# Moving pairs of operand slabs of an MLP to different addresses modulo 256

## The chip, the cores and the metric

The kernel runs on one core of one Trainium2 chip. The metric is the device time of one execution in microseconds (us); lower is better. The kernel before takes 698.64 us (median of 3 runs, 698.64 to 700.39). One more execution was profiled; it took 700.27 us, of which the profile shows a span of 698.4 us. The engines are named as in the profile: PE is the matrix engine (its weight loads are shown apart as PEld), DVE the vector engine, ACT the scalar engine, POOL the general-purpose engine, SP the engine whose queue issues most of the transfers.

## The reference

One layer of a decoder for 512 tokens of width 1024 in float32. Cut to what matters here:

```python
u = rms_norm(h, attn_pre_norm)
proj = u @ w_in                                   # two groups of heads: gated DeltaNet, block attention
mix = concatenate([o_gdn, o_moba]) @ w_out
h = h + rms_norm(mix, attn_post_norm)
f = square(relu(rms_norm(h, mlp_pre_norm) @ w_up)) @ w_down      # the MLP, inner width 4096
h = h + rms_norm(f, mlp_post_norm)
h = h + sigmoid(h @ w_ple_gate) * (p @ w_ple)
```

The change touches only the storage of operands in the MLP (the line with `w_up` and `w_down`) and in the last gate product (`w_ple_gate`).

## The kernel before

**Split operands.** A float32 operand is held as two tiles in the matrix engine's reduced type (F32R in the code, fp32r in the profile): `hi` is a cast of it by ACT, `lo` is the rest, by a subtraction on DVE. `split` (L672 to L677) does this: the cast is L675, the subtraction L676. `mm3` (L181 to L185) makes one product of two such pairs as three matmuls into one accumulator: hi by hi (L182), then hi by lo and lo by hi (both L185). Its first operand `l` is stationary (loaded as weights, 128 columns), its second, `r`, is moving (512 columns as a rule, 256 or 260 in a few places). Every matmul has its own weight load.

**The front part** (to about 262 us) is the input projection and both groups of heads. Its weights are loaded in chunks by `load_w` (L152) into rings of four `hi` and four `lo` tiles of 1040 floats each, one chunk of 8 k-tiles after the other. A tile has 4160 bytes in each partition, 16 times 256 and 64 more, so the tiles of a ring do not all start at the same address modulo 256. In the program as it is allocated the four take the starts 224, 160, 96 and 32 (modulo 256) turn by turn, `hi` and `lo` of one chunk always the same. These weight chunks are the stationary operand of the projections `pc`, `pmk`, `pmq` and `pz`; the moving one is `uT`, which starts at 224 modulo 256. Every slice of these operands that one matmul reads begins a multiple of 512 bytes further on, so it has the same address modulo 256 as its tile.

| operand (front part) | address modulo 256 |
|---|---|
| moving: `uT` hi and lo | 224 |
| stationary, chunk of `pmk2`, `pmq2` | 224 |
| stationary, chunk of `pmk3`, `pmq3` | 160 |
| stationary, chunk of `pmk0`, `pmq0` | 96 |
| stationary, chunk of `pmk1`, `pmq1` | 32 |

`pmk0` to `pmk3` and `pmq0` to `pmq3` are the keys and queries of the second group of heads, 24 matmuls each, in this order. `wv` is the one group of the front with 260 columns: there `uT` is stationary and the weights move, at many different addresses modulo 256 (steps of 16).

**The MLP.** Its operands lie in slabs of 1024 floats (4096 bytes in each partition). The class `Slabs` (L630) keeps a list of free slabs for each of two types: `sf` for float32 (raw weights and intermediate results), `sr` for F32R (all split operands). `more` (L634) makes new ones, `take` takes the first of the list, `give` puts slabs back at its end; so slabs are used in turn, and a slab's next writer waits for the matmuls that read it last. `sr` gets its slabs at three places: R_LEFT = 11 in a pool on the left side of the memory, R_RIGHT = 4 in a pool on the right side once the front's pools are closed (L749), and R_LATE = 12 (L850) over the space of the raw `w_down` tiles and of `f0`, when the main loop is over. The allocator rounds the size of every tile up to a multiple of 32 bytes.

As 4096 is a multiple of 256, all 27 `sr` slabs have the same address modulo 256, namely 224, and so have the moving operands `u2T` and `h2T` (both are in the place of `uT`). The slices that a matmul reads begin at multiples of 512 bytes inside a slab.

Products of this part, all through `mm3`:

- `up` (L757), 32 blocks: stationary is a split pair of `w_up`, moving is `u2T`. The first four blocks run as two halves of 256 columns each, the other 28 with 512. Output tiles are called `pu`.
- `product` (L804), 7 times for each of three quarters of the inner width (a Strassen scheme, 21 products in all): stationary is a split pair of activations `fs`, moving are two split pairs of `w_down`, 24 matmuls of 512. Output tiles are called `pd`. After each product `next_up` runs one block of `up`, so the order on PE is 24 matmuls of `pd`, 24 of `pu`, and so on; one `product` and one `up` take 8 slabs in turn.
- the last quarter, from L885: activations `f_hl` (four split pairs, held from their making to the end) by `w_down` slabs `wd` (8 pairs), 192 matmuls.
- the gate, from L903: stationary is `h2T`, moving are split pairs of `w_ple_gate`, 168 matmuls of 512 and 48 of 256. Output tiles are called `pg`.

The order of instructions on each engine is made by the framework's scheduler from the program order and the dependences. Casts and subtractions for coming products are issued as soon as their slabs come free, one to two products ahead of PE.

Of the kernel before, what the change touches and what calls it, by code (L numbers as in the profile page):

```python
# [10 lines left out]
F32R = mybir.dt.float32r  # L11
# [4 lines left out]
P = 128  # L16
T = 512
NT = T // P
D = 1024
# [11 lines left out]
BLK = 32  # L31
LVL = (32, 64)

F_LEFT, R_LEFT, R_RIGHT, R_LATE = 12, 11, 4, 12


K_ID = 0
# [31 lines left out]
def hybrid_layer(ctx: ExitStack, tc: tile.TileContext, x, p, w_in, w_tok, w_out, w_up, w_down, w_ple, w_gate,  # L69
# [560 lines left out]
    class Slabs:  # L630
# [2 lines left out]

        def more(self, n, pool):  # L634
            for _ in range(n):
                self.free.append(pool.tile([P, D], self.dt, name=f"{self.name}{self.made}"))
                self.made += 1

        def take(self):
# [157 lines left out]
    for g in range(NS):  # L797
        f = F[g % 2]
# [166 lines left out]
```

## Time and profile before

| what | before |
|---|---|
| median of 3 runs | 698.64 us |
| profiled execution | 700.27 us |
| its span | 698.4 us |
| PE busy | 682.5 us (98% of the span) |
| DVE busy | 439.0 us (63%) |
| ACT busy | 324.5 us (46%) |
| front part, 0 to 262 us: PE busy | 256.83 us |
| output projection, 262 to 302 us: PE busy | 38.57 us of 40 |
| first blocks of `up`, 302 to 350 us: PE busy | 47.05 us of 48 |
| Strassen products with `up`, 350 to 595 us: PE busy | 245.00 us of 245 |
| last quarter, 595 to 644 us: PE busy | 47.20 us of 49 |
| gate, 644 to 698 us: PE busy | 47.83 us of 54 |

How to read it: matmuls are pipelined in the profile, a row gives 390 ns for one of 512 columns, but the next one starts about 227 ns after it. So the rate of PE is read from the distance between starts in the timeline, not from the duration in a row. Where PE is busy all the time, every nanosecond between two starts is a nanosecond of the total.

### The profile page before, as it was taken

Reading aid. Unit: us, or ns where it says so; the run is one execution under the profiler, and the core shown is the slowest. Engines: PE = TensorE matmul, PEld = TensorE weight load, DVE = VectorE, ACT = ScalarE, POOL = GpSimd, SP = SyncE. Lnnn points to the kernel's source line nnn. Section 1 sums busy time; section 2 is a strip of 40 time slices with the busy share of each in tenths; the row PEclk is TensorE's granted clock in tenths of the full one; section 3 lists DMA queues with packets and bytes.
Section 4 is the critical chain, followed back from the end, with each engine's and each line's share of the span. In section 5 each row is a group of like instructions: output and inputs, shape, how many; then the busy total and the mean of one; then the engine's idle time right before and its main releaser. Section 6 shows DMA issues by size and latency. Waiting matters only on the chain. (4 is left out here: it accounts for less than half of the span.)

```text
span 698.4 us, 9002 instructions
## 1 busy us (share of the span) xinstructions
PE 682.5 (98%) x3418; PEld 564.8 (81%) x3418; DVE 439.0 (63%) x687; ACT 324.5 (46%) x598; POOL 48.6 (7%) x91
## 2 busy tenths in 40 slices
PE   8999999999999999999999999999999999999897
PEld 5998888888877768789888888888888888678786
DVE  4748889367676655675386456955778756634532
ACT  6536343433466655445265644454335454523311
POOL 1401100000011100230000000000000000032100
PEclk9999999999999999999999999999999999999999
DMA  8732323532102028286004440154211124544421
GB/s 331 301 122 61 101 86 105 114 109 92 31 31 61 31 61 309 112 258 255 31 31 150 122 150 31 61 151 151 90 35 56 61 76 136 184 84 121 122 77 47
DMA packets 38556, 79.24 MB, mean 113 GB/s; under 512 B 9776, under 2 KB 10416, under 8 KB 38512
## 3 DMA queue, kind: packets, MB, share of 16 engines
q1 hardware_dynamic: 36640, 74.98, 32.7%
q0 software_dynamic: 1152, 2.10, 1.9%
q10 hardware_dynamic: 720, 1.57, 0.6%
q8 instruction: 27, 0.44, 0.3%
q14 instruction: 17, 0.14, 0.1%
HBM read 70.51 MB, written 7.08 MB: 111 GB/s over the span
## 5 line engine op out<-in xcount | busy, mean ns | idle before, releaser
L185 PE MATMUL pd<-sr,sr 128*128 128x512 f32 x464 | 143.6, 390 | 0.6 <-DVE sr L676 0.5
L185 PE MATMUL pu<-u2Tl,sr 128*128 128x512 f32 (+1 forms) x288 | 105.4, 366 | 0.7 <-DVE u2Tl L198 0.7
L182 PE MATMUL pu<-u2Th,sr 128*128 128x512 f32 (+1 forms) x288 | 105.4, 366 | 0.0
L185 PE MATMUL pu<-u2Th,sr 128*128 128x512 f32 (+1 forms) x288 | 105.2, 365 | 0.0
L185 PEld LDWEIGHTS pd<-sr,sr 128*128 128x128 f32 x464 | 86.9, 188 | 19.8 <-DVE sr L676 1.7
L182 PE MATMUL pd<-sr,sr 128*128 128x512 f32 x232 | 90.7, 391 | 0.5 <-ACT sr L675 0.5
L676 DVE TENSOR_TENSOR sr<-sf,sr 128x1024 fp32r<-128x1024 f32 x48 | 58.6, 1222 | 38.5 <-ACT sr L675 14.9
L676 DVE TENSOR_TENSOR sr<-wd,sr 128x1024 fp32r<-128x1024 f32 x42 | 51.3, 1222 | 29.6 <-PE pu L185 28.1
L770 ACT ACTIVATE f<-pu 128x512 f32<-128x512 f32 (+1 forms) x36 | 19.9, 552 | 95.7 <-PE pu L185 95.7
L675 ACT CAST sr<-sf 128x1024 fp32r<-128x1024 f32 x48 | 50.3, 1047 | 27.3 <-DMA sf<-in_w_ple_gate 11.9
L185 PEld LDWEIGHTS pu<-u2Tl,sr 128*128 128x128 f32 x288 | 54.3, 189 | 9.7 <-DVE u2Tl L198 0.9
L185 PEld LDWEIGHTS pu<-u2Th,sr 128*128 128x128 f32 x288 | 54.3, 189 | 8.8
L182 PEld LDWEIGHTS pu<-u2Th,sr 128*128 128x128 f32 x288 | 54.3, 189 | 8.6
L675 ACT CAST sr<-wd 128x1024 fp32r<-128x1024 f32 x42 | 44.2, 1051 | 19.4 <-PE pd L185 19.4
L182 PEld LDWEIGHTS pd<-sr,sr 128*128 128x128 f32 x232 | 43.6, 188 | 10.1 <-ACT sr L675 1.4
L182 PE MATMUL pc<-uTh,w_h 128*128 128x512 f32 x96 | 39.3, 409 | 0.0
L185 PE MATMUL pc<-uTh,w_l 128*128 128x512 f32 x96 | 38.6, 402 | 0.0
L185 PE MATMUL pc<-uTl,w_h 128*128 128x512 f32 x96 | 38.5, 401 | 0.0
L825 DVE TENSOR_TENSOR sf<-sf,pd 128x512 f32<-128x512 f32 x28 | 19.1, 685 | 22.2 <-PE pd L185 22.2
L830 DVE TENSOR_TENSOR wd<-wd,wd 128x1024 f32<-128x1024 f32 x24 | 29.3, 1223 | 0.6
L182 PE MATMUL pg<-sr,h2Th 128*128 128x512 f32 (+1 forms) x72 | 27.2, 377 | 0.0
L185 PE MATMUL pg<-sr,h2Th 128*128 128x512 f32 (+1 forms) x72 | 27.0, 376 | 0.0
(421 smaller groups left out, 1324.2 us busy)
## 6 DMA issues: line engine op xcount, KB each, us to landing
sf<-in_w_up SPq DMA_DIRECT2D x32, 512.0 KB, 3.3
wd<-in_w_down SPq DMA_DIRECT2D x24, 512.0 KB, 4.7
w_r<-in_w_in SPq DMA_DIRECT2D x12, 512.0 KB, 3.6
wo_r<-in_w_out SPq DMA_DIRECT2D x8, 512.0 KB, 3.7
sf<-in_w_ple_gate SPq DMA_DIRECT2D x8, 512.0 KB, 4.3
sf<-in_w_down SPq DMA_DIRECT2D x8, 512.0 KB, 4.3
wv_r<-in_w_tok SPq DMA_DIRECT2D x4, 520.0 KB, 6.6
x<-in_x SPq DMA_DIRECT2D x4, 512.0 KB, 6.9
```

What stands on the lines that cost most here:

```text
L182: nc.tensor.matmul(dst, l[0], r[0], start=start, stop=False)
L185: nc.tensor.matmul(dst, a, b, start=False, stop=stop and i == 1)
L675: nc.scalar.copy(hi, src)
L676: nc.vector.tensor_sub(lo, src, hi.bitcast(F32))
L770: nc.scalar.activation(fq[:, side, c0:c1], pt[:, :n], AF.Relu)
L825: add(dst, dst, pts[j])
L830: sub(B[dst + (kk,)], B[x_ + (kk,)], B[y_ + (kk,)])
```

## The change

`R_LEFT` goes from 11 to 10, so that all three groups of `sr` slabs have even sizes (10, 4, 12) and a split pair always takes two neighbours of one group. The second slab of each pair is made wider than the 1024 floats that are used, by the difference of two neighbours in a list of 13 offsets, modulo 256 bytes. The pair behind it thereby starts at another address modulo 256. Nothing else changes: the same instructions on the same shapes, with one slab less.

```diff
-F_LEFT, R_LEFT, R_RIGHT, R_LATE = 12, 11, 4, 12
+F_LEFT, R_LEFT, R_RIGHT, R_LATE = 12, 10, 4, 12
+SKEW = (0, 64, 128, 32, 16, 96, 192, 48, 160, 80, 112, 224, 240)
...
         def more(self, n, pool):
             for _ in range(n):
-                self.free.append(pool.tile([P, D], self.dt, name=f"{self.name}{self.made}"))
+                wide = 0
+                if self.dt == F32R and self.made % 2:
+                    i = self.made // 2
+                    wide = (SKEW[(i + 1) % len(SKEW)] - SKEW[i]) % 256 // 4
+                self.free.append(pool.tile([P, D + wide], self.dt, name=f"{self.name}{self.made}")[:, 0:D])
                 self.made += 1
```

## The prediction

> **What bounds the kernel now.** I read the page first, then busy time by stage, then PE's waits in the MLP, then its timeline. The page and the table by stage (columns: us, then busy us and count of PE, PEld, DVE, ACT, POOL, granted clock, DMA share, GB/s):
>
> ```profile
> PE 682.5 (98%) x3418; PEld 564.8 (81%) x3418; DVE 439.0 (63%) x687; ACT 324.5 (46%) x598; POOL 48.6 (7%) x91
> ...
> 350.00:595.00 245.00, 245.00 (x1083) 202.85 (x1082) 165.15 (x160) 120.38 (x144) 0.00 (x0) 1.00 0.30 94
> 595.00:644.00 49.00, 47.20 (x211) 37.57 (x210) 25.62 (x29) 19.79 (x31) 9.25 (x15) 1.00 0.48 121
> 644.00:698.00 54.00, 47.83 (x234) 39.98 (x232) 19.29 (x28) 10.94 (x18) 2.83 (x5) 0.96 0.30 91
> ```
>
> From 350 to 595 us PE is busy for 245.00 of 245 us at full clock. PE's waits between 302 and 600 us are these two, both before 320 us:
>
> ```profile
> PE pu L185 <- DVE u2Tl L198: 0.7, 1, 0.7
> PE u L206 <- PE pu L185: 0.3, 1, 0.3
> ```
>
> So the MLP costs the number of its matmuls times the distance between two starts, and only a change of that distance, or a new wait, can move the time. The distance is read from the timeline (start, duration, engine, line). Rows of L182 are every third matmul:
>
> ```profile
> 383.21 0.39 PE L182 MATMUL pd<-sr,sr 128*128 128x512 f32 x1
> ...
> 388.65 0.39 PE L182 MATMUL pu<-u2Th,sr 128*128 128x512 f32 x1
> ```
>
> One Strassen product: 24 starts in 5.44 us, 226.7 ns each. All its operands start at 224 modulo 256. The front part has the comparison that this change calls for, the same shape with `uT` moving from 224 and a stationary chunk from other addresses:
>
> ```profile
> 97.10 0.39 PE L182 MATMUL pmk<-uTh,wmk_h 128*128 128x512 f32 x1
> ...
> 100.60 0.39 PE L182 MATMUL pmk<-uTh,wmk_h 128*128 128x512 f32 x1
> ...
> 107.46 0.39 PE L182 MATMUL pmk<-uTh,wmk_h 128*128 128x512 f32 x1
> ...
> 111.58 0.39 PE L182 MATMUL pmk<-uTh,wmk_h 128*128 128x512 f32 x1
> 112.27 0.40 PE L182 MATMUL pmq<-uTh,wmq_h 128*128 128x512 f32 x1
> ...
> 117.15 0.40 PE L182 MATMUL pmq<-uTh,wmq_h 128*128 128x512 f32 x1
> ...
> 124.15 0.39 PE L182 MATMUL pmq<-uTh,wmq_h 128*128 128x512 f32 x1
> ...
> 128.91 0.39 PE L182 MATMUL pmq<-uTh,wmq_h 128*128 128x512 f32 x1
> ```
>
> Call *distance* the start of the next matmul's stationary operand minus the start of the present one's moving operand, modulo 256 (the next weights load while the present matmul runs). The chunks in turn: `pmk1`, stationary at 32, distance 64: 15 starts in 3.50 us, 233.3 ns. `pmk3`, at 160, distance 192: 18 in 4.12 us, 228.9 ns. `pmq0`, at 96, distance 128: 21 in 4.88 us, 232.4 ns. `pmq2`, at 224, distance 0: 21 in 4.76 us, 226.7 ns, as in the MLP. The rate changes with the chunk's tile and comes back with it. Equal addresses are the fastest of the four cases; the others cost 6.7 (64), 5.7 (128) and 2.2 ns (192) more per matmul.
>
> **What the change does to the addresses.** The pads in bytes are 64, 64, 160, 240, 80 in the left group, 96, 112 in the right one, 112, 176, 32, 112, 16, 16 in the late one. Sizes are rounded up to 32, so 240 counts 256, 80 counts 96, 112 counts 128, 176 counts 192 and 16 counts 32. The left group still begins at 224, so its five pairs start at 224, 32, 96, 0, 0. The right group ends where it ended and is 224 bytes longer, so it begins at 0: pairs at 0 and 96. The late group is below it, at 224, 96, 32, 64, 192, 224. They don't all differ: three pairs of the main loop start at 0. `u2T` and `h2T` stay at 224.
>
> Walking the free list through the program (a product takes three pairs, a block of `up` one, of seven in turn) gives the distance of each 512-wide matmul on a slab. Their numbers are from these groups (mean duration overlaps the next matmul):
>
> ```profile
> L185 PE MATMUL pd<-sr,sr 128*128 128x512 f32 x464 | 143.6, 390 | 0.6 <-DVE sr L676 0.5
> L182 PE MATMUL pd<-sr,sr 128*128 128x512 f32 x232 | 90.7, 391 | 0.5 <-ACT sr L675 0.5
> L182 PE MATMUL pu<-u2Th,sr 128*128 128x512 f32 x224 | 87.1, 389 | 0.0
> ...
> L182 PE MATMUL pg<-sr,h2Th 128*128 128x512 f32 x56 | 22.6, 404 | 0.0
> ```
>
> 464 + 232 `pd`, 3 x 224 `pu` and 3 x 56 `pg` are 1536. Of them 261 keep distance 0, 170 get 64, 377 get 128, 103 get 192; 375 get 32 (286 of them `pu`, whose slab is at 0 against `u2T` at 224), 85 get 96, 129 get 160, 36 get 224.
>
> *Priced distances.* 170 x 6.7 + 377 x 5.7 + 103 x 2.2 ns = 1.14 + 2.15 + 0.23 = 3.5 us more, all on PE where it never waits.
>
> *Unpriced distances* (32, 96, 160, 224; 625 matmuls). Upper bound: the dearest row, 6.7 ns each, 4.2 us. Lower bound, a gain: that of a matmul without any overhead. Compare matmuls of 256 and 260 columns:
>
> ```profile
> 302.44 0.28 PE L182 MATMUL pu<-u2Th,sr 128*128 128x256 f32 x1
> ...
> 304.96 0.28 PE L182 MATMUL pu<-u2Th,sr 128*128 128x256 f32 x1
> ...
> 30.08 0.28 PE L182 MATMUL wv<-wv_h,uTh 128*128 128x260 f32 x1
> ...
> 34.40 0.29 PE L182 MATMUL wv<-wv_h,uTh 128*128 128x260 f32 x1
> ```
>
> 21 starts in 2.52 us and 36 in 4.32 us: 120.0 ns both. From 256 to 512 columns 106.7 ns are added, so 512 columns alone are 213.3 ns and 13.3 ns are overhead; 625 x -13.3 = -8.3 us. I take the line between the neighbours that have rows: 32 between 0 and 6.7 (3.3), 96 between 6.7 and 5.7 (6.2), 160 between 5.7 and 2.2 (4.0), 224 between 2.2 and 0 (1.1): 1.24 + 0.53 + 0.52 + 0.04 = 2.3 us. A gain I don't take, because the `wv` rows run over moving addresses in steps of 16, so over all these distances, and show none. For the same reason the 256-wide blocks get no price.
>
> *Casts and subtractions* write to moved slabs. The front's tiles are spread in the same way and cost the same, 1221 against 1222 ns, and both engines have room. So nothing; without that room a few ns times 90 would still be under 1 us.
>
> ```profile
> L161 DVE TENSOR_TENSOR w_l<-w_r,w_h 128x1024 fp32r<-128x1024 f32 x12 | 14.7, 1221 | 15.7 <-ACT w_h L160 15.7
> L676 DVE TENSOR_TENSOR sr<-wd,sr 128x1024 fp32r<-128x1024 f32 x42 | 51.3, 1222 | 29.6 <-PE pu L185 28.1 <-PE pd L185 1.4
> ```
>
> *One slab less.* In the main loop 14 slabs make seven pairs. A cast that ran a slab earlier now waits for the next group of matmuls, at most 5.4 us (24 x 226.7 ns). How far ahead casts run, the seventh product of the first quarter shows:
>
> ```profile
> 399.53 1.06 ACT L675 CAST sr<-wd 128x1024 fp32r<-128x1024 f32 x1
> ...
> 415.85 0.39 PE L182 MATMUL pd<-sr,sr 128*128 128x512 f32 x1
> ```
>
> The cast of its second raw `w_down` tile starts 16.3 us before its first matmul; 5.4 us less is hidden. It is tightest in the last product, when `f_hl` holds three pairs: the cast at 568.90 now waits for the product that ends at 573.6.
>
> ```profile
> 568.90 1.04 ACT L811 CAST sr<-f 128x1024 fp32r<-128x1024 f32 x1
> ...
> 575.50 2.35 DVE L676 TENSOR_TENSOR sr<-wd,sr 128x1024 fp32r<-128x1024 f32 x2
> ...
> 579.08 0.39 PE L182 MATMUL pd<-sr,sr 128*128 128x512 f32 x1
> ```
>
> PE needs them at 579.08, DVE is done with them at 577.85; a cast and a subtraction that move inside this stretch leave about a microsecond. In the last quarter it is on the path:
>
> ```profile
> 590.66 1.05 ACT L675 CAST sr<-sf 128x1024 fp32r<-128x1024 f32 x1
> 595.58 1.05 ACT L675 CAST sr<-sf 128x1024 fp32r<-128x1024 f32 x1 [3.88 <-DMA sf<-in_w_down]
> ...
> 599.06 1.05 ACT L675 CAST sr<-f 128x1024 fp32r<-128x1024 f32 x1
> ...
> 600.16 0.50 PE L182 MATMUL pd<-sr,sr 128*128 128x512 f32 x1 [0.33 <-ACT sr L675]
> ```
>
> The cast of 590.66 now gets a slab that the last `up` block reads until 595.4. It joins the row of casts before the one at 599.06, for which PE waits at 600.16. Queued behind it on ACT is that cast of `f_hl`, on SP the next `w_down` load into the same raw slab. I take one cast, 1.0 us; bounds 0 (another order) and 2 us (a cast and the subtraction behind it).
>
> **Sum.** 3.5 + 2.3 + 1.0 = 6.8 us on PE's path. The profiled execution (700.27, span 698.4) would become 707.1; it stands 1.6 us above the median. On the median: 698.64 + 6.8 = 705.4 us. With the bounds 0 and 4.2, 0 and 2, this case goes from 702.1 to 708.3.
>
> **The rivals.**
>
> *The other side: odd multiples of 32 free the overhead.* If a weight read at distance 32, 96, 160 or 224 no longer meets the moving read, up to 13.3 ns fall away for each of the 625: 698.64 + 3.5 - 8.3 + 1.0 = 694.8 us. It decides from 5.6 ns gained per matmul (3.5 / 625). For it: no 512-wide row has such a distance. Against it: `wv`, above. Chance 0.11. [...]
>
> *Aligned starts.* 256 and 260 columns cost the same, as if a moving read were counted in steps of 128 bytes (32 columns, 13.3 ns) and 224 touched one step too many. 252 moving operands now start at 0: 252 x -13.3 = -3.4 us, 702.0 us in all, 698.7 with the lower bounds. Nothing shows a 512-wide moving read from a multiple of 128. Chance 0.15, a third of it within the measurement.
>
> *No effect.* The front's rates could belong to something else that goes round with the ring, such as ACT or DVE filling it. Then only the slab remains: 698.6 to 699.7. Against it: the rate is steady within a chunk and is the same for `pmk2` and `pmq2`. Chance 0.09. [...]
>
> *Starved casts.* If each of 21 products waited for one cast of 1.05 us: 22 us more. The distances ahead speak against it. Chance 0.03.
>
> **How the numbers follow.** Forecast 0.62. A measurement here can tell 0.3%, 2.1 us. Faster: 0.11 and a little of the aligned case, 0.12. Same: 0.09 of no effect, the third of the aligned case and a little, 0.16. Slower: 0.72. The range 698.5 to 708.3 takes in my case and the aligned and no-effect ones, and leaves out the other side, the starved casts and a few hundredths: 2 in 10.
>
> **What would show it.** After the change `pu` blocks on slabs at 0 (distance 32) should have 226.7 plus 0 to 6.7 ns between starts, those at 96 (distance 128) 232.4. The fifth product of the first quarter has all operands at 0: 226.7 ns there says that only the distance counts, 213 to 216 says that the start itself does. PE should still have no wait from 350 to 595 us, and a longer one near 600. I am wrong if distance 32 is under 226 ns, or if PE waits for casts in the main loop.

## The result

The changed kernel takes 707.17 us (median of 4 runs, 706.84 to 707.5) against 698.73 us (4 runs, 698.64 to 700.39) for the kernel before: a ratio of 1.0115, interval 1.0098 to 1.0133. It is slower by 8.4 us; forecast were 6.8. Run again later, beside four other kernels, it took 707.63 against 699.86 us, a ratio of 1.0120 (1.0101 to 1.0139). The profiled execution after took 707.07 us, its span is 705.3 us, 6.9 more than before.

Below are the first line of the page after, two rows of the table by stage (the same columns as before; the stages end later now), and a row for the stretch of 245 us that was shown of before:

```profile
PE 689.0 (98%) x3418; PEld 564.7 (80%) x3418; DVE 438.7 (62%) x687; ACT 326.1 (46%) x598; POOL 47.8 (7%) x91
```

```profile
350.00:603.00 253.00, 253.00 (x1092) 204.94 (x1092) 167.66 (x162) 124.87 (x148) 0.00 (x0) 1.00 0.28 91
...
652.00:705.00 53.00, 46.32 (x223) 38.10 (x222) 20.36 (x29) 10.85 (x18) 2.83 (x5) 0.95 0.27 81
```

```profile
350.00:595.00 245.00, 245.00 (x1057) 198.48 (x1057) 164.56 (x159) 120.55 (x142) 0.00 (x0) 1.00 0.27 87
```

The number to look at is the count. In the same 245 us, with PE busy for all of them at full clock, it starts 1057 matmuls where it started 1083 before: 231.8 ns each in place of 226.2 (a few of each count are records cut by the edges, so these are means of the stretch, not exact rates). Instructions, busy share and clock are as before. No wait was added in this stretch; most matmuls start a little later.

Single blocks show it in the timeline of the changed kernel. Each pair of neighbouring rows spans 24 matmuls:

```profile
378.70 0.40 PE L183 MATMUL pu<-u2Th,sr 128*128 128x512 f32 x1
...
384.30 0.39 PE L183 MATMUL pd<-sr,sr 128*128 128x512 f32 x1
...
389.89 0.39 PE L183 MATMUL pu<-u2Th,sr 128*128 128x512 f32 x1
...
395.47 0.40 PE L183 MATMUL pd<-sr,sr 128*128 128x512 f32 x1
...
400.92 0.39 PE L183 MATMUL pu<-u2Th,sr 128*128 128x512 f32 x1
```

From 378.70 to 384.30 runs a block of `up` on a slab at 0 (distance 32): 5.60 us, 233.3 ns each. From 389.89 to 395.47 one on a slab at 96 (distance 128): 5.58 us, 232.5 ns. From 395.47 to 400.92 runs the fifth product of the first quarter, with all its operands at 0: 5.45 us, 227.1 ns.

Pairing every 512-wide matmul after 300 us with the addresses of the program as allocated gives the means below. "Counted" and "more, predicted" are the prediction's count and price; the last three columns are measured, and "more" is over 226.7 ns.

| distance | counted | more, predicted | n | mean ns to the next start | more, measured |
|---|---|---|---|---|---|
| 0 | 261 | 0 | 259 | 228.7 (median 227) | 2.0 |
| 64 | 170 | 6.7 | 169 | 233.1 | 6.4 |
| 128 | 377 | 5.7 | 375 | 232.3 | 5.6 |
| 192 | 103 | 2.2 | 106 | 229.4 | 2.7 |
| 32 | 375 | 3.3 | 373 | 233.2 | 6.5 |
| 96 | 85 | 6.2 | 86 | 233.3 | 6.6 |
| 160 | 129 | 4.0 | 123 | 233.8 | 7.1 |
| 224 | 36 | 1.1 | 35 | 232.4 | 5.7 |

Where the time went, stage by stage. "Rate" is the growth of the time from one start to the next (where it is at most 262 ns, so without stalls), summed over the stage; the last column is how much the stage itself grew in the two profiled executions:

| stage | rate, us | stage, us |
|---|---|---|
| up to the first product (350.55, then 350.72) | 0.5 | 0.2 |
| products with `up` (to 595.40, then 601.31) | 5.7 | 5.7 |
| last quarter (to 644.08, then 649.74) | 0.7 | -0.2 |
| gate (to the last matmul, 693.61, then 700.50) | 0.8 | 1.2 |
| together | 7.7 | 6.9 |

In the main loop the two columns agree to 0.1 us: the rate accounts for the whole growth there.

The waits of PE from 590 to 655 us, before and after:

```profile
PE h L881 <- DMA sf<-hd: 0.7, 1, 0.7
PE pd L182 <- ACT sr L675: 0.5, 2, 0.3
PE pd L185 <- DVE sr L676: 0.5, 1, 0.5
```

```profile
PE pd L183 <- ACT sr L680: 1.5, 2, 0.9
```

```profile
601.27 1.05 ACT L680 CAST sr<-sf 128x1024 fp32r<-128x1024 f32 x1 [0.56 <-PE pu L186]
...
606.68 1.04 ACT L680 CAST sr<-f 128x1024 fp32r<-128x1024 f32 x1
```

```profile
607.78 0.50 PE L183 MATMUL pd<-sr,sr 128*128 128x512 f32 x1 [0.58 <-ACT sr L680]
...
610.13 0.50 PE L183 MATMUL pd<-sr,sr 128*128 128x512 f32 x1 [0.93 <-ACT sr L680]
```

The rows are ACT's and PE's, all after. The missing slab does what was described: the cast at 601.27 waits for the last `up` block, the cast of `f_hl` starts 5.37 us after the start of the quarter in place of 3.66 (599.06 - 595.40), and PE waits for it at 607.78. But these waits cost 1.5 us, against 1.0 us for casts and subtractions before, and the 0.7 us that PE stood for a transfer of the residual (`hd`) in this stage before did not come. The stage is not longer than before.

### The profile page after: what moved, and what is told of

It reads as the page before. It is cut to its first block, busy times and chain, and to the rows that moved or that the text cites. A ratio compares the mean times of both kernels' runs of the same rounds, so it can differ in the third digit from the quotient of the medians.

```text
span 705.3 us, 9012 instructions
## 1 busy us (share of the span) xinstructions
PE 689.0 (98%) x3418; PEld 564.7 (80%) x3418; DVE 438.7 (62%) x687; ACT 326.1 (46%) x598; POOL 47.8 (7%) x91
## 5 line engine op out<-in xcount | busy, mean ns | idle before, releaser
L186 PE MATMUL pd<-sr,sr 128*128 128x512 f32 x464 | 145.2, 394 | 0.0
L183 PE MATMUL pu<-u2Th,sr 128*128 128x512 f32 (+1 forms) x288 | 106.5, 370 | 0.0
L186 PE MATMUL pu<-u2Th,sr 128*128 128x512 f32 (+1 forms) x288 | 106.3, 369 | 0.0
L183 PE MATMUL pd<-sr,sr 128*128 128x512 f32 x232 | 91.6, 395 | 1.5 <-ACT sr L680 1.5
L186 PE MATMUL pg<-sr,h2Tl 128*128 128x512 f32 (+1 forms) x72 | 27.0, 376 | 0.0
```

What stands on the lines that cost most here:

```text
L183: nc.tensor.matmul(dst, l[0], r[0], start=start, stop=False)
L186: nc.tensor.matmul(dst, a, b, start=False, stop=stop and i == 1)
```

## The experiments

Eight kernels ran, in two groups, each group on one chip beside the kernel before: 699.62 us (697.12 to 702.04) in the first, 699.86 (697.75 to 700.93) in the second. All but the last group's repeat of the change are edits of the kernel before.

**One slab less, nothing moved.**

```diff
-F_LEFT, R_LEFT, R_RIGHT, R_LATE = 12, 11, 4, 12
+F_LEFT, R_LEFT, R_RIGHT, R_LATE = 12, 10, 4, 12
```

> The kernel before with R_LEFT = 10 and no pads: 14 slabs in the main loop, all starts at 224 modulo 256 as before. Theory (the time of the change comes from the distance between the next stationary and the present moving operand): every 512-wide matmul of the MLP keeps 226.7 ns between starts, and only the term for one slab less is left. The prediction took 1.0 us for it, 699.7 us; from the trace after, in which the last quarter is not longer than before, I now expect 0, 698.7 us. Rival (the smaller pool is what costs): 705 to 707 us, with waits of PE for casts or subtractions in the main loop.

Measured: 701.08 us, ratio 1.0024 (1.0009 to 1.0040), so 0.6 to 2.8 us more. The rival (705 to 707 us) falls. The trace doesn't show where the 1.5 us between the medians come from:

```profile
350.00:595.00 245.00, 245.00 (x1083) 202.88 (x1082) 165.44 (x160) 122.16 (x144) 0.00 (x0) 1.00 0.29 92
```

```profile
596.56 0.39 PE L182 MATMUL pd<-sr,sr 128*128 128x512 f32 x1
...
603.28 0.50 PE L182 MATMUL pd<-sr,sr 128*128 128x512 f32 x1 [0.85 <-ACT sr L675]
...
643.74 0.39 PE L182 MATMUL pg<-sr,h2Th 128*128 128x512 f32 x1
```

The main loop has its 1083 matmuls. In the last quarter PE waits for a cast for 0.85 us at 603.28, but that quarter lasts 47.18 us, where before it lasted 48.68 (595.40 to 644.08). The span, 698.3, is that of before (698.4). The clock may make the difference: each execution has its mean granted clock on record, and none of these 12 reached 0.998, where 9 of the 29 of the kernel before did. Taken at 0.996 alone, the medians are 700.7 us (6 executions) and 700.3 (11).

**Slabs moved by whole multiples of 256 bytes.**

```diff
+                wide = 64 if self.dt == F32R and self.made % 2 and self.made < 14 else 0
+                self.free.append(pool.tile([P, D + wide], self.dt, name=f"{self.name}{self.made}")[:, 0:D])
```

(also `R_LEFT` 10)

> R_LEFT = 10 and every second slab of the left and right group 256 bytes wider: slabs are moved against one another by as much as in the change and the pools are longer, but all starts stay equal modulo 256. Theory (only the distance modulo 256 counts): as with R_LEFT = 10 alone, 698.7 us, 226.7 ns between starts. Rival (moved or padded slabs cost by themselves, or the distance counts modulo 512 or more): towards 707 us, 230 to 233 ns between starts.

Measured: 699.93 us, ratio 1.0005 (0.9988 to 1.0023).

```profile
350.00:595.00 245.00, 245.00 (x1083) 202.89 (x1082) 165.43 (x160) 123.11 (x145) 0.00 (x0) 1.00 0.29 93
```

1083 again. That slabs are moved, are wider than what is used and no longer lie side by side costs nothing; the place modulo 256 is what counts. It has the same 14 slabs as the kernel above, and its ratio's interval holds 1 and ends at 1.6 us, so the price of the slab lies between nothing and about 1.6 us. The two traces, whose last quarters are shorter than before (47.18 and 47.04 us against 48.68), don't confirm a wait that would make it up.

**`hi` where it was, `lo` 64 bytes on.** Slabs take turns, `hi` at 224 and `lo` at 32; `u2T` and `h2T` stay at 224. Of the three matmuls of a product one then moves `lo` and one loads `lo`.

```diff
+                wide = 0 if self.dt != F32R else 48 if self.made % 2 else 16
+                self.free.append(pool.tile([P, D + wide], self.dt, name=f"{self.name}{self.made}")[:, 0:D])
```

(also `R_LEFT` 10)

> R_LEFT = 10, every lo slab starts 64 bytes behind its hi slab modulo 256 (hi at 224, lo at 32), all pairs alike. This tells which stationary operand counts, the next matmul's (loaded while the present one runs) or the present one's own. A product runs hi by hi, hi by lo, lo by hi. Theory (next): in the Strassen products all distances stay 0, 226.7 ns; in the up blocks one of three is 64, the matmul before the lo stationary, 228.9 ns in the mean: 224 x 6.6 ns = 1.5 us, with 56 gate matmuls at 192 (0.1 us) 1.6 us more than R_LEFT = 10 alone, 700.3 us. Rival (own): products have 0, 192 and 64, 229.6 ns in the mean, 696 / 3 x 8.9 ns = 2.1 us more on top, 702.4 us, and the slow matmul of an up block is that on the lo stationary itself.

Measured: 704.73 us, ratio 1.0072 (1.0051 to 1.0094). Both forecasts started from 698.7 us for 14 slabs, and on this chip that kernel took 701.08. Over it the measured time is 3.7 us more; the first theory has 1.6, the second 3.7. So the time speaks against the first alone, and the second could have been believed. The rates refute both. In the 245 us of the main loop 1060 matmuls start:

```profile
350.00:595.00 245.00, 245.00 (x1060) 198.93 (x1059) 164.43 (x159) 120.63 (x142) 0.00 (x0) 1.00 0.27 87
```

```profile
384.72 0.39 PE L182 MATMUL pd<-sr,sr 128*128 128x512 f32 x1
...
390.26 0.40 PE L182 MATMUL pu<-u2Th,sr 128*128 128x512 f32 x1
...
395.82 0.39 PE L182 MATMUL pd<-sr,sr 128*128 128x512 f32 x1
```

A product takes 5.54 us for 24, 230.8 ns; a block of `up` 5.56 us, 231.7 ns. The time from one start to the next, sorted by kind, is 231.7 ns where `lo` moves, 229.8 where `lo` is stationary and 232.1 where both are `hi` in `pd`; in `pu` it is 233.7 where `lo` is stationary, 230.5 and 230.2 for the other two. None is at 226.7. In `pd` the order of `hi` and `lo` makes every distance to the next stationary operand 0, and by the second theory the matmuls with both `hi` are at 0 there; neither is at the 226.7 ns that this would give. So a price per distance, which the forecast was added up from, does not describe this kernel. One displaced operand in three slows all three. The theory that took its place: starts come evenly, every 226.7 ns (226, 227, 227 in whole ns), when all operands of several matmuls in a row agree modulo 256, and a displaced one breaks this rhythm for some matmuls.

**Everything at 224, the front too.** If that holds, the front gains when its weight chunks all start at 224. The tiles of its rings become 1088 floats (4352 bytes, 17 times 256), and a small unused tile moves the operand of the output projection to 224 as well.

```diff
-        hi = wp.tile([P, 1040], F32R, tag="hi", bufs=4, name=f"{name}_h")
-        lo = wp.tile([P, 1040], F32R, tag="lo", bufs=4, name=f"{name}_l")
+        hi = wp.tile([P, 1088], F32R, tag="hi", bufs=4, name=f"{name}_h")
+        lo = wp.tile([P, 1088], F32R, tag="lo", bufs=4, name=f"{name}_l")
...
+    actB.tile([P, 16], F32, name="apad")
```

(also `R_LEFT` 10, to make room)

> The opposite of the change, in the front part: R_LEFT = 10, no pads on slabs, hi and lo tiles of the weight ring 1088 floats wide instead of 1040 (4352 bytes, 17 times 256), and one unused tile of 16 floats so that the operands of the output projection start at 224 too. Now all stationary and moving operands of the split products start at 224 modulo 256. Theory: the 577 matmuls of the front and of the output projection at distances 64, 128 and 192 go from 233, 232 and 229 ns to 226.7: 193 x 6.5 + 192 x 5.6 + 192 x 2.4 ns = 2.8 us less than R_LEFT = 10 alone, a little less where PE waits in the front: 696 to 696.7 us. Rival (the front's rates come from the ring's other work, not from addresses): 698.7 us, the same 233 ns for pmk1.

Measured: 698.15 us, ratio 0.9983 (0.9965 to 1.0000); against the kernel with 14 slabs alone, on the same chip, 2.9 us less, as forecast. The chunk `pmk1`, 233.3 ns before:

```profile
96.94 0.39 PE L182 MATMUL pmk<-uTh,wmk_h 128*128 128x512 f32 x1
...
101.02 0.39 PE L182 MATMUL pmk<-uTh,wmk_h 128*128 128x512 f32 x1
```

18 starts take 4.08 us, 226.7 ns each. Over all 512-wide matmuls of split products the mean is 227.3 ns. The dear rows of the front that the prediction read its prices from were indeed a matter of address: they go when the addresses agree.

**Only the moving operands displaced.** 15 slabs at 224 as before, `u2T` and `h2T` 32 bytes on, at 0. Products keep equal addresses; blocks of `up` have a constant distance of 224, the gate one of 32.

```diff
+        at = 0 if name == "uT" else 8
+        return tuple(act.tile([P, KT * T + 64], F32R, tag=f"A{n}", bufs=1, name=f"{name}{n}")[:, at:at + KT * T]
+                     .rearrange("p (k t) -> p k t", k=KT) for n in "hl")
```

> The kernel before with its 11 + 4 + 12 slabs, all at 224, but u2T and h2T moved by 32 bytes, to 0 modulo 256. No slab is moved and none taken away; the up blocks run at the one distance 224 throughout, the gate at 32, the products of activations by w_down stay at 0. Theory (unequal starts keep PE from the 226.7 ns rhythm): up 232.5 to 233.5 ns, 672 x 6.3 ns = 4.2 us, gate 168 x 6.5 ns = 1.1 us, in all 5 us more than before, and pd at 226.7. Rival (what costs is that pairs differ from one another, not a fixed difference): no change. Rival (reads that begin at a multiple of 128 are faster): up towards 213 to 216 ns, up to 9 us less.

Measured: 703.99 us, ratio 1.0065 (1.0051 to 1.0078), 4.1 us more, where 5 were forecast.

```profile
384.38 0.40 PE L182 MATMUL pd<-sr,sr 128*128 128x512 f32 x1
...
385.08 0.40 PE L182 MATMUL pd<-sr,sr 128*128 128x512 f32 x1
...
385.78 0.39 PE L182 MATMUL pd<-sr,sr 128*128 128x512 f32 x1
...
386.46 0.39 PE L182 MATMUL pd<-sr,sr 128*128 128x512 f32 x1
387.14 0.39 PE L182 MATMUL pd<-sr,sr 128*128 128x512 f32 x1
...
389.86 0.40 PE L182 MATMUL pu<-u2Th,sr 128*128 128x512 f32 x1
```

```profile
395.46 0.40 PE L182 MATMUL pd<-sr,sr 128*128 128x512 f32 x1
```

The block of `up` from 389.86 to 395.46 takes 5.60 us, 233.3 ns each, with `u2T` at 0: a moving operand from a multiple of 256 is not cheaper by itself. Over all 672 such matmuls the mean is 233.4 ns, in the gate 233.3. In the product ahead of it every third start is shown: three matmuls take 0.70, 0.70, 0.68, 0.68 us. After this displaced block the rate is slow for at least six matmuls (233 ns each) though all addresses agree, and only then is at 226.7. The mean of 228.7 at distance 0 in the table of the result holds such a settling, not always as long: in the changed kernel the product at 395.47 has one start after 232 ns and is then at 226.7.

**Everything at 224 with all 15 slabs.** As two above, with `R_LEFT` 11 again; the room comes from keeping a scratch tile of squares, whose values nothing reads, in 16 bits.

```diff
-        jk = m_.tile([P, 512], F32, tag="njk", bufs=1, name=f"{name}j")
+        jk = m_.tile([P, 512], mybir.dt.bfloat16, tag="njk", bufs=1, name=f"{name}j")
```

> All operands of split products at 224 as in the run before with all equal, but with 11 slabs on the left again (15 in the main loop); the room comes from keeping the unread squares of sum_half in a 16-bit tile. Theory: before less 2.8 us, a little less where PE waits in the front: ratio 0.996 to 0.9965. Rival (the fifteenth slab is worth nothing and the front's gain is noise): ratio 0.999 to 1.0.

Measured: 697.8 us, ratio 0.9974 (0.9960 to 0.9988): the lowest median of all kernels here, 2.1 us under the kernel before on the same chip and 9.8 under the changed one.

```profile
300.92 0.28 PE L182 MATMUL pu<-u2Th,sr 128*128 128x256 f32 x1
```

```profile
350.00:595.00 245.00, 245.00 (x1083) 202.88 (x1082) 165.32 (x161) 120.69 (x145) 0.00 (x0) 1.00 0.29 94
```

The first block of `up` starts at 300.92, where it started at 302.44: the gain is 1.5 us ahead of the MLP, and the main loop is untouched. That is less than the 2.8 us of the forecast: `pmq` goes from 230.6 to 226.7 ns, but `pc` only from 231.2 to 228.8 and `pz` from 231.1 to 230.6.

**The change again,** on this chip.

> The change itself once more beside the others on one chip: 7 to 8.5 us more than before; against R_LEFT = 10 alone the addresses are then 6 to 8 us of it.

Measured: 707.63 us, ratio 1.0120 (1.0101 to 1.0139). That is 7.8 us more than before, as forecast; moving `u2T` and `h2T` alone cost 4.1 us.

**Small steps.** Pairs of the main loop sliced 4 to 240 bytes into wider slabs, `hi` and `lo` alike, `u2T` at 224; 14 slabs.

```diff
+                at = (1, 2, 4, 12, 28, 44, 60)[self.made // 2] if self.dt == F32R and self.made < 14 else 0
+                wide = 64 if at else 0
+                self.free.append(pool.tile([P, D + wide], self.dt, name=f"{self.name}{self.made}")[:, at:at + D])
```

> R_LEFT = 10, the seven pairs of the main loop moved by 4, 8, 16, 48, 112, 176 and 240 bytes from 224. Theory (any unequal start breaks the rhythm): up blocks at distances 4 to 240 all at 229 to 234 ns, none under 226.7. Rival (the memory is read in pieces of 16 or 32 bytes, and a start inside the same piece is as good as equal): 226.7 ns at 4, 8 and perhaps 16 bytes, 229 to 234 ns at 48 to 240. Rival (some finer distance frees the overhead): 213 to 222 ns at one of them.

Measured: 706.24 us (one run). Blocks of `up` have one distance each, and the rows show three of them, 24 matmuls from `pu` to the next block:

```profile
367.39 0.39 PE L182 MATMUL pu<-u2Th,sr 128*128 128x512 f32 x1
...
372.92 0.39 PE L182 MATMUL pd<-sr,sr 128*128 128x512 f32 x1
...
400.84 0.39 PE L182 MATMUL pu<-u2Th,sr 128*128 128x512 f32 x1
...
406.32 0.40 PE L182 MATMUL pd<-sr,sr 128*128 128x512 f32 x1
...
422.98 0.40 PE L182 MATMUL pu<-u2Th,sr 128*128 128x512 f32 x1
...
428.56 0.39 PE L182 MATMUL pu<-u2Th,sr 128*128 128x512 f32 x1
```

The slab 8 bytes past `u2T` gives 5.53 us (230.4 ns), 240 bytes past it, which is 16 bytes short of it, 5.48 us (228.3), 4 bytes past it 5.58 us (232.5). The other distances give means of 233.0 (16), 233.1 (48), 233.1 (112) and 230.0 ns (176). So the finest step that the type allows, one float, already costs nearly the full price, while a stationary operand 16 bytes behind costs next to nothing: one of these blocks (at 556 us) runs at 226.7 ns throughout, though others of the same distance (at 339.63 and 595.28) stay at 228.4 and 228.7. Both rivals fall, since 4 and 8 bytes are not free and nothing is under 226.7 ns; the theory fails at 240, which it had at 229 or more. These distances show neither a threshold nor a smooth curve.

## Why the prediction was nearly right

*Slower, on PE's rate, with no new wait in the main loop:* right. 1057 against 1083 matmuls in 245 us show it, and the kernel moved by multiples of 256, with 1083 again, shows that the address modulo 256 is the cause. From the first product to the last quarter the main loop lasts 244.80 to 244.85 us in the profiles of all five kernels that keep its operands at one address modulo 256, with 14 slabs or 15; it lasts 249.5 (`u2T` moved), 249.9 (`lo` moved), 250.1 (small steps) and 250.6 us (the change, both times).

*The addresses and the counts:* right, to 6 matmuls in any class.

*Priced distances, 3.5 us:* right. With the measured prices and counts: 169 x 6.4 + 375 x 5.6 + 106 x 2.7 ns = 3.5 us. The front's rows did carry over.

*Unpriced distances, 2.3 us:* the term that was mis-sized. "I take the line between the neighbours that have rows" made 32 a cheap case (3.3 ns) because 0 is, and 224 because 0 and 192 are. Measured are 373 x 6.5 + 86 x 6.6 + 123 x 7.1 + 35 x 5.7 ns = 4.1 us, the upper bound that the prediction gave as 4.2. Distance 0 is not the end of a slope. At 4 bytes the price is already 5.7 ns (232.4).

*Equal distances cost nothing:* nearly. 259 x 2.0 ns = 0.5 us are the settling after displaced matmuls, which a price per matmul cannot hold.

*One slab less, 1.0 us:* the order of work was as described, down to the cast of `f_hl` behind the row, but the stage did not grow in the trace. By the two kernels that take the slab away without changing any address modulo 256 it is between 0 and about 1.6 us (1.0024 and 1.0005), so the bounds of 0 and 2 hold and the value is not settled.

The sum by measured terms is 3.5 + 4.1 + 0.5 = 8.1 us, with the slab at nothing; the medians differ by 8.4 and 7.8 us. In the profiled pair it is 6.9, since before's stood 1.5 us above the median of 698.73. The forecast was 1.8 us low at the unpriced distances and 0.5 at the settling, and up to 1.0 us high at the slab; errors of opposite sign brought it nearer than its terms were.

*The rivals.* "Odd multiples of 32 free the overhead" falls: distance 32 costs 6.5 ns more, not 13.3 less. "Aligned starts" falls twice: the product with all operands at 0 runs at 227.1 ns, and with `u2T` at 0 blocks run at 233.3. "No effect" falls with the count of 1057 and with 233.3 ns against 226.7 on the same shape in one loop; that a weight read meets a moving read is not shown by this, only that the addresses matter. "Starved casts" falls: PE is busy for 253.00 of 253 us from 350 to 603.

*The model beneath it.* The forecast gave each matmul a price by the distance from its moving operand to the next stationary one. The kernel with `lo` moved refutes that: in its products it predicts 226.7 ns and 230.8 were measured. The sum held because in the change, as in the front, `hi` and `lo` of a pair move alike and runs of 12 or 24 matmuls mostly share one distance, so that the price of a run could be read as one per matmul; that the change is laid out so was luck for this model. That a rhythm holds only while all starts agree fits the other kernels, but not the blocks 16 bytes behind, which reach 226.7 ns, and it doesn't say why 64 bytes behind costs only 2.7 ns. It is argued from the gaps between starts, not shown by a view of the memory. What in the chip makes the rhythm stays open.

## What to carry to other kernels

Where PE is busy without a gap, look at the time from one start to the next: 1083 against 1057 in the same 245 us is nearly the whole of this result, and no wait and no busy share shows it. Give all fp32r operands of one stream, moving and stationary, `hi` and `lo`, the same address modulo 256 (tile sizes that are multiples of 256 bytes do it); spreading them cost 2 to 7 ns for each 512-column matmul here, and making them agree in the front gained 1.5 us ahead of the MLP. And do not interpolate a price between a special case and its neighbours: bound it by the dearest row until a row of its own exists.

## What the runs showed that was not expected

*A rate that settles.* At equal addresses starts come evenly, every 226.7 ns; after the blocks with `u2T` moved they need at least six matmuls to come back to it (0.70, 0.70, then 0.68 us for three, above). Displaced blocks have patterns of their own: 80 bytes behind (distance 176) the gaps repeat 229, 226, 229, 236 ns.

*A half clock for one stretch.* In the gate PE waits before transposes (`h`), and then runs at half speed. After:

```profile
665.01 0.75 PE L886 MATMUL h<-ident,sf 128*128 128x128 f32 x4 [1.94 <-DVE sf L924]
...
665.98 0.63 PE L186 MATMUL pg<-sr,h2Th 128*128 128x512 f32 x1
...
667.69 0.63 PE L186 MATMUL pg<-sr,h2Tl 128*128 128x512 f32 x1
```

Four matmuls in 1.71 us are 427 ns each, twice the 213.3 ns that the prediction worked out for 512 columns alone. Two windows of this profile, the slow stretch and the 3.4 us ahead of it (columns as in the table by stage):

```profile
665.40:668.75 3.35, 3.35 (x11) 2.68 (x9) 0.69 (x1) 0.59 (x1) 0.00 (x0) 0.50 0.62 210
661.97:665.38 3.41, 1.00 (x8) 0.82 (x9) 1.98 (x3) 1.17 (x2) 0.00 (x0) 1.00 0.63 144
```

The granted clock is 0.50 in the first. In both profiles, before and after, some eight matmuls are slow in this way, about 1.6 us together, and the clock record has 0.50 for 3.41 us; eight times 427 ns are 3.4 us. In the 3.41 us ahead of the stretch, at a granted clock of 1.00, PE was busy for 1.35 us before and for 1.00 us after. The profiles of the kernels with everything at 224 and 14 slabs, and with `u2T` moved, have no such stretch: their mean granted clock is 0.999, where the other eight have 0.993 to 0.997, and 3.41 us at 0.50 alone take 0.0024 off. Yet PE waits before transposes in them too, for 2.1 and 2.0 us at one time, against 1.65 us before and 1.94 after. So the length of one such wait does not decide it; what does, no run here tested. The granted clock goes with part of the scatter between single executions (697.12 to 702.04 us for the kernel before): of those 29 executions, the 9 with a mean granted clock of 0.998 or more have a median of 697.7 us, the other 20 one of 700.4.
